# One-layer S5 trunk: 1/rms interleaved with the powers, decays ahead of the outer products, three pools opened in another order

## The chip, the core and the metric

The kernel runs on one core of a Trainium2 chip. It has a matrix engine (TensorE, PE in the rows), a vector engine (VectorE, DVE), an engine for functions of one input (ScalarE, ACT), GpSimd (POOL), and queues that issue DMAs: most are issued by SyncE (SP), some by GpSimd. Each engine works through its own instructions in the order in which they stand. The metric is the device time of one execution in microseconds (us); lower is better.

## The reference

With DEPTH = 1 there is one layer on 2048 frames of 1024 values: an S5 mixer, a squared-ReLU MLP, a gate with a per-layer input embedding, and a last norm.

```python
def rmsnorm(x, gain):  # x * rsqrt(mean(x*x) + 1e-6) * gain

h = rmsnorm(x, norm_mix)
# S5, for each of 64 groups of 16 channels, 64 complex states:
#   a = exp(lam*dt);  state[t] = a*state[t-1] + B u[t];  y = Re(C state) + d*u
y = gelu(s5(h));  a, g = split(y @ w_glu)
x = x + a * sigmoid(g)
x = x + relu(rmsnorm(x, norm_ffn) @ w1)**2 @ w2
x = x + (p @ ple_w) * sigmoid(rmsnorm(x, norm_ple) @ ple_gate_w)
return rmsnorm(x, norm_final)
```

All is float32. Large products run as three products of a high and a low part each: the high part is a cast by ScalarE (`h_`), the low part a subtraction by VectorE (`l_`).

## The kernel before

The 2048 frames are two halves of 1024 (`hb` 0 and 1), the channels eight octets of 8 groups. The stages, in order of time:

- **Prologue.** VectorE works out a, its powers 1 to 8 (`pw_r`, `pw_i`, lines 410 to 423) and from power 8 the decays `al[:, 0]`; `stat_steps` (line 180) gives 1/rms of half 0 from sums of squares that ScalarE made, in 14 small instructions on 128x8 values. `decay_steps` (line 434) squares `al` seven times: `sq`, then the real part, then the imaginary part. `scan` reads `al[:, 0]` to `al[:, 6]`.
- **S5 of half 0** (line 882 on). An octet has the outer products `gm` (`make_w`) and `vm` (`make_v`): each is a product with the real powers, one with the imaginary powers, and their sum. VectorE makes them whole (3 instructions of 128x1024) for octets in `W_DVE` and `V_DVE`, GpSimd in halves (6 instructions of 128x512) for the others. `norm` multiplies the frames by 1/rms, `turn` and `turn_w` transpose, `sums` multiplies into `xs`, which lies in PSUM, `scan` runs the recurrence on VectorE. Octets go in pairs: both scans take turns, and the lists `PLAN0` to `PLAN2` say after which step of the scan the other engines' work is issued. `make_k` needs `vm` of its octet. `Ple` is the product of p and `ple_w`, whose pieces (`pp`, `po`) go beside the scans; `rest` makes the low part `plo` of the transposed p.
- **GLU of half 0** with S5 of half 1 beside it, then **the MLP of half 0** (`mlp`): products `up` with w1, then `dn` with w2, each in units that `run` issues with loads and casts some units ahead. Then **the gate** (`gate`). The same for half 1.

The S5 stage and the MLP stand inside `tc.manual_schedule`: the named engines get their instructions in the written order. Outside such a block a scheduler sets the order. It also lets code that is written after the block (the first gate weights `raw_gw`, `w_gw`) stand between the block's instructions.

Buffers come from pools that are opened and closed like a stack, from both ends of SBUF. A pool opened where another was closed takes its memory, and its tiles wait for the last use of the old ones. `open_residual` (line 1544) opens the pools of the second part of the MLP and of the gate over the pools `uw` and `ur` of `up` (`ur` holds the raw w1 blocks `rawu`), at the end of `up`. In half 1 `ur` is opened over these again:

```python
wp = right.enter_context(...)      # 9 x 4 KB, over uw
rawp = right.enter_context(...)    # 4 x 2 KB raw weights of gate and GLU
tmps[-1] = right.enter_context(...)  # 3 x 2 KB
aps.append(right.enter_context(...))  # 7 x 2 KB and 4 KB of g_fin
```

Of the kernel before, what the change touches and what calls it, by code (L numbers as in the profile page):

```python
# [9 lines left out]
F32 = mybir.dt.float32  # L10
# [3 lines left out]
ALU = mybir.AluOpType  # L14
# [16 lines left out]
NOCT = 8  # L31
# [7 lines left out]
def trunk(  # L39
# [24 lines left out]
    pe, dve, act, pool, sp = nc.tensor, nc.vector, nc.scalar, nc.gpsimd, nc.sync  # L64
# [30 lines left out]
    const = ctx.enter_context(tc.tile_pool(name="const", bufs=1))  # L95
# [25 lines left out]

    ident = const.tile([P, P], F32, name="ident")
    make_identity(nc, ident)
    al = const.tile([P, 8, NOCT, 2, 2, 4], F32, name="al")
    carry = const.tile([P, 2, 32], F32, name="carry")
    g_ffn = const.tile([P, KT], F32, name="g_ffn")
    g_ple = const.tile([P, KT], F32, name="g_ple")
# [62 lines left out]
    pr0 = tmp.enter_context(tc.tile_pool(name="pr0", bufs=1, side="right"))  # L190
# [16 lines left out]
    for i, c in enumerate((c_re, c_im)):  # L207
# [9 lines left out]
    sq = small.tile([P, NOCT, 2, 4], F32, name="sq", bufs=1)  # L217
# [6 lines left out]
        out=k_d[:].rearrange("(a b) h r -> (b h) a r", b=8)[:, :, 0:7 * H], in_=zpad)  # L224
# [37 lines left out]
    ss0 = stat_squares(0, xs0[:10])  # L262
# [74 lines left out]
    pw_r = par.tile([P, 9, G], F32, name="pw_r")  # L337
    pw_i = par.tile([P, 9, G], F32, name="pw_i")
# [71 lines left out]
    for lo, n in ((1, 1), (2, 2), (4, 4)):  # L410
        q1 = pr0.tile([P, 4, G], F32, tag="q1", name=f"q1_{lo}", bufs=2)[:, :n]
        q2 = pr0.tile([P, 4, G], F32, tag="q2", name=f"q2_{lo}", bufs=2)[:, :n]
        q3 = pr0.tile([P, 4, G], F32, tag="q3", name=f"q3_{lo}", bufs=2)[:, :n]
        q4 = pr0.tile([P, 4, G], F32, tag="q4", name=f"q4_{lo}", bufs=2)[:, :n]
        ar, ai = pw_r[:, 1:n + 1], pw_i[:, 1:n + 1]
        br = pw_r[:, lo:lo + 1].broadcast_to([P, n, G])
        bi = pw_i[:, lo:lo + 1].broadcast_to([P, n, G])
        mul(q1, ar, br)
        mul(q2, ai, bi)
        mul(q3, ar, bi)  # L420
        mul(q4, ai, br)
        sub(pw_r[:, lo + 1:lo + 1 + n], q1, q2)
        add(pw_i[:, lo + 1:lo + 1 + n], q3, q4)


    for e in range(2):
        ls = slice(e * S, e * S + S)
        pr = pw_r[ls, 8].rearrange("p (o i e) -> p e o i", e=2, i=4)[:, e]
        pi = pw_i[ls, 8].rearrange("p (o i e) -> p e o i", e=2, i=4)[:, e]
        for r_ in range(2):  # L430
            dve.tensor_copy(out=al[ls, 0, :, 0, r_], in_=pr)
            ts(al[ls, 0, :, 1, r_], pi, 1.0 - 2 * r_, ALU.mult)

    def decay_steps():
        for k in range(7):
            re = al[:, k, :, 0]
            mul(sq, al[:, k, :, :, 0], al[:, k, :, :, 0])
            yield
            tt(al[:, k + 1, :, 0], sq[:, :, 0].unsqueeze(2).broadcast_to([P, NOCT, 2, 4]),
               sq[:, :, 1].unsqueeze(2).broadcast_to([P, NOCT, 2, 4]), ALU.subtract)  # L440
            yield
            stt(al[:, k + 1, :, 1], re, 2.0, al[:, k, :, 1], ALU.mult, ALU.mult)
            yield

    rs0 = []
    for _ in stat_steps(0, ss0, rs0):
        pass
    startup.close()
    tmp.close()


    beside = []

    def tick(n=None):

        for _ in range(n or TICK):
            if beside:
                g = beside.pop(0)
                if next(g, StopIteration) is not StopIteration:
                    beside.append(g)  # L460

    W_DVE, V_DVE = (0,), (0, 2, 4, 6)
    TICK = 4

    class Octet:

# [45 lines left out]
        def outer(self, name, sl, za, zb, on_pool):  # L512

            eng = pool if on_pool else dve
            a_ = self.tile(name, (P, 8, 8, H))
            n = 4 if on_pool else 8
            for j in range(0, 8, n):
                js = slice(j, j + n)
                b_ = self.tile(f"{name}b{j}", (P, n, 8, H), tag="pa" if on_pool else "tm")
                for t, w, z in ((a_[:, js], pw_r, za), (b_, pw_i, zb)):  # L520
                    eng.tensor_tensor(out=t, in0=self.powers(w, sl)[:, js], in1=self.spread(z)[:, js], op=ALU.mult)
                    if not on_pool:
                        tick()
# [357 lines left out]
    ples = [Ple(j // 2, j % 2) for j in range(4)]  # L881
    with tc.manual_schedule(engines=MANUAL):
# [64 lines left out]
        Ple.load_weights()  # L947
        ples[0].load()
        ples[1].load()
        Ple.weights()  # L950
        a, b = pairs[0]
        a.make_w()
        b.make_w()
        octs[2].make_w()
        b.make_v()
        a.turn_w()
        ples[0].turn(True)
        a.norm(True)
        beside += [decay_steps()]
        a.turn()  # L960
        b.turn_w()
        b.norm()
        a.sums()
        b.turn()
        b.sums()
        a.make_v()
        while beside:
            tick(1)
        diagonal()
        Ple.weights_rest()  # L970
        ple_rest(0)
# [4 lines left out]
        for k in range(NP):  # L976
            a, b = 2 * k, 2 * k + 1
# [19 lines left out]
        a, b = pairs[-1]  # L997
# [28 lines left out]
    tmps, aps = [], []  # L1026
# [511 lines left out]
    right = ctx.enter_context(ExitStack())  # L1538
# [5 lines left out]
    def open_residual(hb):  # L1544

        nonlocal xp, wp, rawp, g_fin, ps_tp
        tops.close()
        xp = left.enter_context(tc.tile_pool(name=f"xp{hb}", bufs=8, reuse_waits="tile"))
        wp = right.enter_context(tc.tile_pool(name=f"wp{hb}", bufs=9, side="right", reuse_waits="tile"))
        rawp = right.enter_context(tc.tile_pool(name=f"rawp{hb}", bufs=4, side="right", reuse_waits="tile"))  # L1550
        tmps[-1] = right.enter_context(tc.tile_pool(name=f"tp_{hb}", bufs=3, side="right", reuse_waits="tile")), 512
        aps.append(right.enter_context(tc.tile_pool(name=f"ap_{hb}", bufs=7, side="right", reuse_waits="tile")))
        g_fin = aps[-1].tile([P, D], F32, name=f"g_fin{hb}", bufs=1)
        sp.dma_start(out=g_fin, in_=norm_final.partition_broadcast(P))

# [50 lines left out]
```

## Time and profile before

| | us |
|---|---|
| time, median of 3 runs | 2131.78 |
| lowest and highest run | 2127.62 to 2133.33 |
| the profiled execution's own time | 2130.64 |
| its span, first to last instruction | 2128.9 |
| PE busy | 1993.3 (94%) |
| DVE busy | 1387.4 (65%) |
| ACT busy | 887.9 (42%) |
| POOL busy | 427.0 (20%) |

The page names an instruction by its line, engine and operation, then output<-inputs, then the shape and how many were merged into the row. Idle time stands in brackets with what ended it. The mean granted clock of TensorE over the span is 0.984 of full speed. The time outside the span is 2130.64 - 2128.9 = 1.7 us.

### The profile page before, as it was taken

Reading aid. Unit: us, or ns where it says so; the run is one execution under the profiler, and the core shown is the slowest. Engines: PE = TensorE matmul, PEld = TensorE weight load, DVE = VectorE, ACT = ScalarE, POOL = GpSimd, SP = SyncE. Lnnn points to the kernel's source line nnn. Section 1 sums busy time; section 2 is a strip of 40 time slices with the busy share of each in tenths; the row PEclk is TensorE's granted clock in tenths of the full one; section 3 lists DMA queues with packets and bytes.
Section 4 is the critical chain, followed back from the end, with each engine's and each line's share of the span. In section 5 each row is a group of like instructions: output and inputs, shape, how many; then the busy total and the mean of one; then the engine's idle time right before and its main releaser. Section 6 shows DMA issues by size and latency. Waiting matters only on the chain.

```text
span 2128.9 us, 28570 instructions
## 1 busy us (share of the span) xinstructions
PE 1993.3 (94%) x9750; PEld 1655.5 (78%) x9750; DVE 1387.4 (65%) x2592; ACT 887.9 (42%) x1769; POOL 427.0 (20%) x388
## 2 busy tenths in 40 slices
PE   2788989988999999999999999979999999999997
PEld 1677778776888888888888788867888888888876
DVE  9997587759666666875664722377666657555455
ACT  4675444335333345354443511253333355444443
POOL 5563011123322212522300000022322200000000
PEclk9899999999999999999999999989999999999999
DMA  5677644342444469999832711224444598665112
GB/s 169 191 216 208 198 129 139 100 139 84 153 154 161 145 220 354 373 358 344 274 137 79 269 53 40 85 94 153 159 149 159 172 356 303 206 195 192 39 50 89
DMA packets 241955, 377.35 MB, mean 177 GB/s; under 512 B 23681, under 2 KB 106641, under 8 KB 241809
## 3 DMA queue, kind: packets, MB, share of 16 engines
q1 hardware_dynamic: 234576, 352.46, 49.5%
q0 software_dynamic: 7232, 23.08, 3.0%
q8 instruction: 76, 1.25, 0.2%
q14 instruction: 71, 0.57, 0.1%
HBM read 261.21 MB, written 114.23 MB: 176 GB/s over the span
## 4 chain that ended last, share of the span: by engine, by line
PE 72%; DVE 14%; issue 4%; ACT 4%; DMA 3%; POOL 3%; SPq 0%; DVEq 0%; ACTq 0%; POOLq 0%
PE dn L1376 26%; PE up L1284 25%; PE glu L1046 3%; PE glu L1047 3%; PE glu L1048 3%; PE gt L1046 2%; PE gt L1047 2%; PE gt L1048 2%; DVE tm L72 2%; DVE es L72 2%; DVE xs L72 1%; DVE wu L72 1%; DMA rawu<-in_mlp_w_dram 1%; ACT xs L668 1%; PE glu L850 1%
## 5 line engine op out<-in xcount | busy, mean ns | idle before, releaser
L1284 PE MATMUL up<-h_s,wu 128*128 128x512 f32 x1280 | 407.9, 392 | 8.4 <-DVE ev L72 7.9
L1376 PE MATMUL dn<-h_dw,h_da 128*128 128x512 f32 x896 | 349.1, 390 | 0.0
L1376 PE MATMUL dn<-l_dw,h_da 128*128 128x512 f32 x896 | 348.7, 389 | 0.3 <-DVE l_dw L72 0.3
L1376 PE MATMUL dn<-h_dw,l_da 128*128 128x512 f32 x896 | 348.7, 389 | 0.0
L72 DVE TENSOR_TENSOR l_da<-da,h_da 128x512 fp32r<-128x512 f32 x224 | 183.2, 818 | 178.5 <-ACT h_da L1174 178.4
L1284 PEld LDWEIGHTS up<-h_s,wu 128*128 128x128 f32 x1280 | 242.0, 189 | 61.7 <-DVE ev L72 9.2
L1284 PE MATMUL up<-l_s,wu 128*128 128x512 f32 x640 | 251.0, 392 | 12.4 <-DVE l_s L72 12.4
L72 DVE TENSOR_TENSOR wu<-rawu,wu 128x512 fp32r<-128x512 f32 x224 | 164.3, 747 | 112.1 <-ACT wu L1272 111.7
L1174 ACT CAST h_da<-da 128x512 fp32r<-128x512 f32 x224 | 139.0, 621 | 232.8 <-PE dn L1376 211.7
L1046 PE MATMUL glu<-w_glu,ah_y 128*128 128x512 f32 x492 | 196.1, 399 | 6.2 <-ACT w_glu L734 5.2
L1376 PEld LDWEIGHTS dn<-l_dw,h_da 128*128 128x128 f32 x896 | 168.2, 188 | 35.5 <-DVE l_dw L72 0.8
L1047 PE MATMUL glu<-w_glu,ah_y 128*128 128x512 f32 x492 | 193.9, 394 | 1.6 <-DVE w_glu L72 1.6
L1376 PEld LDWEIGHTS dn<-h_dw,h_da 128*128 128x128 f32 x896 | 168.2, 188 | 34.9
L1376 PEld LDWEIGHTS dn<-h_dw,l_da 128*128 128x128 f32 x896 | 168.2, 188 | 34.8
L1270 POOL TENSOR_TENSOR rawu<-rawu,rawu 128x512 f32<-128x512 f32 x96 | 134.2, 1412 | 299.4 <-DVE wu L72 299.4
L1048 PE MATMUL glu<-w_glu,al_y 128*128 128x512 f32 x492 | 193.5, 394 | 0.0
L1284 PE MATMUL up<-ah_f,wu 128*128 128x512 f32 x512 | 171.8, 397 | 7.3 <-ACT wu L1272 7.0
L1272 ACT CAST wu<-rawu 128x512 fp32r<-128x512 f32 x224 | 132.2, 620 | 91.4 <-POOL rawu L1270 63.4
L72 DVE TENSOR_TENSOR l_dw<-dw,h_dw 128x512 fp32r<-128x512 f32 x224 | 161.0, 719 | 11.0 <-ACT h_dw L1174 9.3
L1295 ACT COPY ev<-up 128x512 f32<-128x512 f32 x96 | 56.3, 586 | 247.0 <-PE up L1284 247.0
L1174 ACT CAST h_dw<-dw 128x512 fp32r<-128x512 f32 x224 | 138.1, 617 | 48.5 <-POOL dw L1361 45.8
L1284 PEld LDWEIGHTS up<-l_s,wu 128*128 128x128 f32 x640 | 121.0, 189 | 38.9 <-DVE l_s L72 14.2
(309 smaller groups left out, 3334.9 us busy)
## 6 DMA issues: line engine op xcount, KB each, us to landing
da<-h_d SPq DMA_DIRECT2D x224, 256.0 KB, 5.0
dw<-in_mlp_w_dram SPq DMA_DIRECT2D x192, 256.0 KB, 5.1
rawu<-in_mlp_w_dram SPq DMA_DIRECT2D x64, 512.0 KB, 3.8
h_d<-ev SPq DMA_DIRECT2D x96, 256.0 KB, 2.1
h_d<-hs SPq DMA_DIRECT2D x96, 256.0 KB, 2.1
dw<-t_d SPq DMA_DIRECT2D x96, 256.0 KB, 4.7
t_d<-dw SPq DMA_DIRECT2D x64, 256.0 KB, 5.1
raw_glu<-in_ssm_w_glu_dram SPq DMA_DIRECT2D x59, 256.0 KB, 4.5
```

Of the source, the lines that this page charges most:

```text
L72: return dve.tensor_tensor(out=o, in0=a, in1=b, op=op)
L668: act.copy(dd[c * S:(c + 1) * S, :, e], self.es[e * S:(e + 1) * S, c])
L850: pe.matmul(out=pf, lhsT=lhs[:, cs_], rhs=wl if i == 1 else wh, start=k == 0 and i == which[0], stop=False)
L1046: pe.matmul(out=ps, lhsT=lh, rhs=rh, start=first, stop=False)
L1047: pe.matmul(out=ps, lhsT=lh, rhs=rl, start=False, stop=False)
L1048: pe.matmul(out=ps, lhsT=ll, rhs=rh, start=False, stop=last)
L1174: act.copy(h_, src)
L1270: pool.tensor_tensor(out=src, in0=src, in1=other, op=ALU.add)
L1272: act.copy(w_[:, 0], src)
L1284: pe.matmul(out=ps, lhsT=lhs, rhs=rhs, start=i in FIRST_IN_CHAIN and k == n == 0, stop=k == 3 and n == 2, skip_group_check=True)
L1295: act.copy(ev[g, i], y_ if i == 5 else x_)
L1376: pe.matmul(out=ps, lhsT=lhs[:, cs_], rhs=rhs, start=i in FIRST_IN_CHAIN and fp == n == 0, stop=fp == NPAIR - 1 and n == 2, skip_group_che ...
```

## The change

Four things are changed in the prologue, and one further on.

1. The six instructions per power round and the 14 of 1/rms take turns on VectorE (`power_steps`, `stat_steps`), instead of powers, then `al[:, 0]`, then 1/rms.
2. The decays (`decays`) are written before all outer products, and not a few at a time between VectorE's outer products by `tick`. They end at `al[:, 6]`; `al` is one entry smaller. The real part of the last one is made by GpSimd, which thus stands ahead of GpSimd's first outer product. Two copies of `al[:, 0]` become one for each half of the lanes.
3. Octet 0 is normalized by ScalarE and not by VectorE, and this, the transposes of p and of octet 0 stand before `turn_w` of octet 0 (and so before `gm` of octet 0 is waited for) on ScalarE and TensorE. The casts of `ple_w` (`plwh`) stand after octet 1's `turn_w`.
4. In `open_residual` the pool of 7 buffers `ap_` is opened ahead of `rawp` and `tp_`.

```diff
-    al = const.tile([P, 8, NOCT, 2, 2, 4], F32, name="al")
+    al = const.tile([P, 7, NOCT, 2, 2, 4], F32, name="al")
...
+    def decays():
+        for e in range(2):
...
+            dve.tensor_copy(out=al[ls, 0, :, 0], in_=pr.unsqueeze(2).broadcast_to([S, NOCT, 2, 4]))
+            for r_ in range(2):
+                ts(al[ls, 0, :, 1, r_], pi, 1.0 - 2 * r_, ALU.mult)
+        for k in range(6):
             mul(sq, al[:, k, :, :, 0], al[:, k, :, :, 0])
+            stt(al[:, k + 1, :, 1], al[:, k, :, 0], 2.0, al[:, k, :, 1], ALU.mult, ALU.mult)
+            (pool if k == 5 else dve).tensor_tensor(
+                out=al[:, k + 1, :, 0], in0=sq[:, :, 0].unsqueeze(2).broadcast_to([P, NOCT, 2, 4]),
+                in1=sq[:, :, 1].unsqueeze(2).broadcast_to([P, NOCT, 2, 4]), op=ALU.subtract)
 
-    for _ in stat_steps(0, ss0, rs0):
-        pass
+    with tc.manual_schedule(engines={mybir.EngineType.Activation, mybir.EngineType.DVE}):
+        steps_ = [power_steps(), stat_steps(0, ss0, rs0)]
+        while steps_:
+            steps_ = [g for g in steps_ if next(g, StopIteration) is not StopIteration]
...
-        Ple.weights()
         a, b = pairs[0]
+        decays()
         a.make_w()
         b.make_w()
         octs[2].make_w()
         b.make_v()
+        a.norm()
+        ples[0].turn(True)
+        a.turn()
         a.turn_w()
-        ples[0].turn(True)
-        a.norm(True)
-        beside += [decay_steps()]
-        a.turn()
+        b.norm()
         b.turn_w()
-        b.norm()
+        Ple.weights()
         a.sums()
...
         wp = right.enter_context(tc.tile_pool(name=f"wp{hb}", bufs=9, side="right", reuse_waits="tile"))
+        aps.append(right.enter_context(tc.tile_pool(name=f"ap_{hb}", bufs=7, side="right", reuse_waits="tile")))
         rawp = right.enter_context(tc.tile_pool(name=f"rawp{hb}", bufs=4, side="right", reuse_waits="tile"))
         tmps[-1] = right.enter_context(tc.tile_pool(name=f"tp_{hb}", bufs=3, side="right", reuse_waits="tile")), 512
-        aps.append(right.enter_context(tc.tile_pool(name=f"ap_{hb}", bufs=7, side="right", reuse_waits="tile")))
```

VectorE in the prologue, from the first outer product of octet 0 on, before (`gm`, `vm`: outer products of octet 0; `xn_0`: its normalized frames; `y_x`: 1/rms; `sq`, `al`: decays):

```order
L521 TENSOR_TENSOR gm_0_546<-pw_r,zz 128x1024
L89 SCALAR_TENSOR_TENSOR y_x_505<-q_x_502,y_x_500 128x8
L521 TENSOR_TENSOR gmb_0_0_547<-pw_i,zz 128x1024
L524 TENSOR_TENSOR gm_0_546<-gm_0_546,gmb_0_0_547 128x1024
L85 TENSOR_SCALAR xn_0_605<-xl_0_514,y_x_505 128x8x16 x8
L521 TENSOR_TENSOR vm_0_695<-pw_r,y_199 128x1024
L72 TENSOR_TENSOR sq<-al 128x64
L72 TENSOR_TENSOR al<-sq 128x8x8
L89 SCALAR_TENSOR_TENSOR al<-al 128x8x8
L72 TENSOR_TENSOR sq<-al 128x64
L521 TENSOR_TENSOR vmb_0_0_696<-pw_i,y_200 128x1024
```

The same place of the changed kernel, from the last decays on:

```order
L89 SCALAR_TENSOR_TENSOR al<-al 128x8x8
L445 TENSOR_TENSOR al<-sq 128x8x8
L72 TENSOR_TENSOR sq<-al 128x64
L89 SCALAR_TENSOR_TENSOR al<-al 128x8x8
L517 TENSOR_TENSOR gm_0_553<-pw_r,zz 128x1024
L517 TENSOR_TENSOR gmb_0_0_554<-pw_i,zz 128x1024
L518 TENSOR_TENSOR gm_0_553<-gm_0_553,gmb_0_0_554 128x1024
L517 TENSOR_TENSOR vm_0_714<-pw_r,y_199 128x1024
L517 TENSOR_TENSOR vmb_0_0_715<-pw_i,y_200 128x1024
L518 TENSOR_TENSOR vm_0_714<-vm_0_714,vmb_0_0_715 128x1024
```

The eight instructions of `xn_0` are gone from VectorE, and no decay stands between the outer products. GpSimd's six instructions each for `gm_1`, `gm_2` and `vm_1` stand as before, but behind one `al<-sq` that waits for VectorE's last `sq`.

SyncE in half 1, where the GLU ends and the MLP begins, before (`raw_glu_b_k`: raw GLU weights of block b; `rawu`: raw w1 blocks):

```order
L1037 DMA raw_glu_3_5_12340<-in_ssm_w_glu_dram 128x2x256
L1037 DMA raw_glu_3_6_12345<-in_ssm_w_glu_dram 128x2x256
L1037 DMA raw_glu_3_7_12350<-in_ssm_w_glu_dram 128x2x256
L1257 DMA rawu_0_0_12696<-in_mlp_w_dram 128x4x256
L1257 DMA rawu_0_1_12698<-in_mlp_w_dram 128x4x256
L1257 DMA rawu_1_0_12700<-in_mlp_w_dram 128x4x256
L1257 DMA rawu_1_1_12702<-in_mlp_w_dram 128x4x256
```

And in the changed kernel, a block and a half of weights earlier:

```order
L1027 DMA raw_glu_2_3_12048<-in_ssm_w_glu_dram 128x2x256
L1247 DMA rawu_0_0_12694<-in_mlp_w_dram 128x4x256
L1027 DMA raw_glu_2_4_12053<-in_ssm_w_glu_dram 128x2x256
L1247 DMA rawu_0_1_12696<-in_mlp_w_dram 128x4x256
L1247 DMA rawu_1_0_12698<-in_mlp_w_dram 128x4x256
L1247 DMA rawu_1_1_12700<-in_mlp_w_dram 128x4x256
L1027 DMA raw_glu_2_5_12058<-in_ssm_w_glu_dram 128x2x256
```

The four loads of the first two w1 blocks moved ahead of eleven loads of GLU weights; `ur` now lies over buffers of `ap_`.

SyncE in half 0, where the MLP ends and the gate begins, before (`raw_gw`: raw gate weights; six of the first eight stand some 300 instructions earlier; `ppl`: pieces of p's product):

```order
L1362 DMA t_d_103<-dw_0_4_15_10157 128x512
L1037 DMA raw_gw_0_6_10615<-in_ple_gate_w_dram 128x512
L1037 DMA raw_gw_0_7_10620<-in_ple_gate_w_dram 128x512
L1453 DMA ppl_0_0_10625<-pp_d 128x512
L1453 DMA ppl_0_1_10659<-pp_d 128x512
```

And in the changed kernel:

```order
L1352 DMA t_d_103<-dw_0_4_15_10155 128x512
L1027 DMA raw_gw_0_0_10583<-in_ple_gate_w_dram 128x512
L1027 DMA raw_gw_0_1_10588<-in_ple_gate_w_dram 128x512
L1027 DMA raw_gw_0_2_10593<-in_ple_gate_w_dram 128x512
L1027 DMA raw_gw_0_3_10598<-in_ple_gate_w_dram 128x512
L1443 DMA ppl_0_0_10623<-pp_d 128x512
L1443 DMA ppl_0_1_10657<-pp_d 128x512
L1027 DMA raw_gw_0_4_10603<-in_ple_gate_w_dram 128x512
L1027 DMA raw_gw_0_5_10608<-in_ple_gate_w_dram 128x512
L1027 DMA raw_gw_0_6_10613<-in_ple_gate_w_dram 128x512
L1027 DMA raw_gw_0_7_10618<-in_ple_gate_w_dram 128x512
```

All eight raw gate weights of the first block now stand here, behind the last load and store of the MLP; ScalarE's casts and VectorE's subtractions of them moved along. In half 1 they stand among the loads of the sixth of the seven `dn` products.

## Rows read from the trace of the kernel before

**Rows 1.** The page, busy time of the engines (share of the span, instructions).
```profile
PE 1993.3 (94%) x9750; PEld 1655.5 (78%) x9750; DVE 1387.4 (65%) x2592; ACT 887.9 (42%) x1769; POOL 427.0 (20%) x388
```

**Rows 2.** Windows of 50 us: busy time (instructions) by engine, granted clock, DMA.
```profile
50.00:100.00 50.00, 34.47 (x276) 28.84 (x278) 49.45 (x127) 26.83 (x65) 25.79 (x23) 0.89 0.57 155
...
1650.00:1700.00 50.00, 50.00 (x223) 41.39 (x222) 32.19 (x49) 16.44 (x30) 11.57 (x9) 1.00 0.48 161
```

**Rows 3.** Timeline of VectorE, 18 to 210 us: start, duration, instruction, shape, count.
```profile
30.69 0.42 DVE L72 TENSOR_TENSOR pw_i<-q,q 128x256 f32<-128x256 f32 x1
...
35.02 1.03 DVE L86 TENSOR_SCALAR v_x<-s 128x8 f32<-128x8 f32 x1
...
48.70 2.01 DVE L524 TENSOR_TENSOR gm<-gm,gmb 128x1024 f32<-128x1024 f32 x1
50.63 5.41 DVE L85 TENSOR_SCALAR xn<-xl,y_x 128x128 f32<-128x128 f32 x8
55.96 1.21 DVE L521 TENSOR_TENSOR vm<-pw_r,y 128x1024 f32<-128x1024 f32 x1
57.09 0.21 DVE L72 TENSOR_TENSOR sq<-al 128x64 f32<-128x64 f32 x1
...
57.73 0.23 DVE L72 TENSOR_TENSOR sq<-al 128x64 f32<-128x64 f32 x1
...
62.10 1.04 DVE L72 TENSOR_TENSOR sq<-al 128x64 f32<-128x64 f32 x1
...
70.48 2.49 DVE L72 TENSOR_TENSOR plwl<-plw,plwh 128x512 fp32r<-128x512 f32 x4
...
74.09 2.34 DVE L72 TENSOR_TENSOR tm<-al,xs 128x1024 f32<-128x1024 f32 x2
...
84.74 1.28 DVE L72 TENSOR_TENSOR plo<-tpp,ph 128x512 fp32r<-128x512 f32 x2
...
93.03 2.31 DVE L72 TENSOR_TENSOR tm<-al,xs 128x1008 f32<-128x1008 f32 x2
...
207.83 0.17 DVE L85 TENSOR_SCALAR h_x<-v_x 128x8 int32<-128x8 int32 x1
```

**Rows 4.** Timeline of GpSimd, 30 to 95 us.
```profile
31.42 1.11 POOL L521 TENSOR_TENSOR gm<-pw_r,zz 128x512 f32<-128x512 f32 x1 [14.21 <-ACT y L386]
...
45.35 2.16 POOL L521 TENSOR_TENSOR vm<-pw_r,y 128x512 f32<-128x512 f32 x1
...
54.04 1.32 POOL L524 TENSOR_TENSOR vm<-vm,vmb 128x512 f32<-128x512 f32 x1
...
82.94 0.60 POOL L815 DMA_DIRECT2D pp_d<-po  x1 [15.07 <-ACT po L813]
...
93.55 1.28 POOL L524 TENSOR_TENSOR vm<-vm,vmb 128x512 f32<-128x512 f32 x1
```

**Rows 5.** Timeline of ScalarE, 59 to 84 us.
```profile
59.58 2.45 ACT L491 ACTIVATE xn<-xl,y_x 128x128 f32<-128x128 f32 x8
...
82.55 1.07 ACT L795 CAST ph<-tpp 128x512 fp32r<-128x512 f32 x2
```

**Rows 6.** Timeline of TensorE where `up` begins: half 0, then half 1.
```profile
467.67 1.04 PE L1067 MATMUL tpx_f<-ident,x 128*128 128x128 f32 x8
...
475.16 1.91 PE L1213 MATMUL tpu<-ident,x 128*128 128x128 f32 x16
...
1381.85 1.04 PE L1067 MATMUL tpx_f<-ident,x 128*128 128x128 f32 x8
1388.46 0.80 PE L1284 MATMUL up<-ah_f,wu 128*128 128x512 f32 x1 [5.57 <-ACT wu L1272]
...
1393.48 1.91 PE L1213 MATMUL tpu<-ident,x 128*128 128x128 f32 x16
```

**Rows 7.** Timeline of SyncE's queue and of TensorE at the gate of half 0.
```profile
1074.62 0.91 SPq L1037 DMA_DIRECT2D raw_gw<-in_ple_gate_w_dram  x2
...
1106.44 0.47 PE L1046 MATMUL gt<-w_gw,ah_g 128*128 128x512 f32 x1
```

**Rows 8.** The tile `raw_gw`: us from the issue of a load to its landing.
```profile
DMA to landing us min/median/max: 2.5/4.5/6.8
```

More of the change, by code (lines that the diff above doesn't have):

```diff
@@ L407, in diagonal @@
         mul(dg, dl.unsqueeze(2).broadcast_to([P, H, H]), mask16.unsqueeze(1).broadcast_to([P, H, H]))
[L410 to L423, printed above, removed]
@@ L426, in trunk, with power_steps @@
[L426 to L436, printed above, removed]
-            mul(sq, al[:, k, :, :, 0], al[:, k, :, :, 0])
[L438 to L443, printed above, removed]
+    def power_steps():
+        for lo, n in ((1, 1), (2, 2), (4, 4)):
+            q1 = pr0.tile([P, 4, G], F32, tag="q1", name=f"q1_{lo}", bufs=2)[:, :n]
+            q2 = pr0.tile([P, 4, G], F32, tag="q2", name=f"q2_{lo}", bufs=2)[:, :n]
+            q3 = pr0.tile([P, 4, G], F32, tag="q3", name=f"q3_{lo}", bufs=2)[:, :n]
+            q4 = pr0.tile([P, 4, G], F32, tag="q4", name=f"q4_{lo}", bufs=2)[:, :n]
+            ar, ai = pw_r[:, 1:n + 1], pw_i[:, 1:n + 1]
+            br = pw_r[:, lo:lo + 1].broadcast_to([P, n, G])
+            bi = pw_i[:, lo:lo + 1].broadcast_to([P, n, G])
+            mul(q1, ar, br)
+            yield
+            mul(q2, ai, bi)
+            yield
+            mul(q3, ar, bi)
+            yield
+            mul(q4, ai, br)
+            yield
+            sub(pw_r[:, lo + 1:lo + 1 + n], q1, q2)
+            yield
+            add(pw_i[:, lo + 1:lo + 1 + n], q3, q4)
+            yield
@@ new lines, in decays @@
+    def decays():
+        for e in range(2):
+            ls = slice(e * S, e * S + S)
+            pr = pw_r[ls, 8].rearrange("p (o i e) -> p e o i", e=2, i=4)[:, e]
+            pi = pw_i[ls, 8].rearrange("p (o i e) -> p e o i", e=2, i=4)[:, e]
+            dve.tensor_copy(out=al[ls, 0, :, 0], in_=pr.unsqueeze(2).broadcast_to([S, NOCT, 2, 4]))
+            for r_ in range(2):
+                ts(al[ls, 0, :, 1, r_], pi, 1.0 - 2 * r_, ALU.mult)
+        for k in range(6):
+            mul(sq, al[:, k, :, :, 0], al[:, k, :, :, 0])
+            stt(al[:, k + 1, :, 1], al[:, k, :, 0], 2.0, al[:, k, :, 1], ALU.mult, ALU.mult)
+            (pool if k == 5 else dve).tensor_tensor(
+                out=al[:, k + 1, :, 0], in0=sq[:, :, 0].unsqueeze(2).broadcast_to([P, NOCT, 2, 4]),
+                in1=sq[:, :, 1].unsqueeze(2).broadcast_to([P, NOCT, 2, 4]), op=ALU.subtract)
@@ L445, in trunk @@
     rs0 = []
-    for _ in stat_steps(0, ss0, rs0):
-        pass
+    with tc.manual_schedule(engines={mybir.EngineType.Activation, mybir.EngineType.DVE}):
+        steps_ = [power_steps(), stat_steps(0, ss0, rs0)]
+        while steps_:
+            steps_ = [g for g in steps_ if next(g, StopIteration) is not StopIteration]
     startup.close()
     tmp.close()
[L452 to L460, printed above, removed]
@@ L462, in trunk @@
     W_DVE, V_DVE = (0,), (0, 2, 4, 6)
-    TICK = 4
     class Octet:
@@ L521, in outer @@
                     eng.tensor_tensor(out=t, in0=self.powers(w, sl)[:, js], in1=self.spread(z)[:, js], op=ALU.mult)
-                    if not on_pool:
-                        tick()
                 eng.tensor_tensor(out=a_[:, js], in0=a_[:, js], in1=b_, op=ALU.add)
-                if not on_pool:
-                    tick()
             return a_
@@ L966, in trunk @@
         a.make_v()
-        while beside:
-            tick(1)
         diagonal()
```

## The prediction

> **What bounds the kernel now.** The first view to read is the page's line of busy times: TensorE works 94% of the span, VectorE 65% [rows 1]. A share of 94% says that most edits on other engines are worth nothing, and that a gain must come from the stretches in which TensorE waits. The windows of 50 us show which these are. From 1650 to 1700 TensorE is busy for all 50.00 us; from 50 to 100, in the S5 stage of half 0, it is busy for 34.47 and VectorE for 49.45 [rows 2]. There VectorE is the bound, and TensorE's later work starts when VectorE has its scans done. So a microsecond taken from VectorE ahead of its first scan step (`tm` at 74.09) is a microsecond of the whole, as long as nothing else comes late at that scan.
>
> The third view is VectorE's timeline of that stretch, read beside GpSimd's. VectorE's busy time there is partly not its own. The tiny 1/rms instruction at 35.02 takes 1.03 where one of the same shape takes 0.17 at 207.83; a decay `sq` takes 1.04 at 62.10 and 0.21 at 57.09; a sum `gm` 2.01 at 48.70, a product of that size 1.21 at 55.96; and the eight pieces of `xn` 5.41 at 50.63 [rows 3], which ScalarE makes for the next octet in 2.45 [rows 5]. GpSimd was at its outer products then, and its own instruction took 2.16 at 45.35 where the first took 1.11 [rows 4]. 2.16 is 1.11 and about one product of VectorE: the two engines take turns, one whole instruction each. An instruction that reads xs in PSUM is not touched: `tm` takes 2.31 for two at 93.03, with GpSimd's sum at 93.55 beside it, and 2.34 at 74.09 [rows 3, 4]. So a small VectorE instruction costs 1 us, not 0.2, wherever GpSimd has a product waiting, and moving the small ones ahead of GpSimd's first product is the core of this change.
>
> The Trainium skill (SBUF — State Buffer, section Who interferes with whom) says that a VectorE instruction with two SBUF inputs contends with a GpSimd instruction that reads SBUF, that the pair of ports is held for the full instruction, and that at most one SBUF input outside the 2-port modes doesn't contend; the slow `gm` and the untouched `tm` above agree. By this rule the products of the two engines never lie beside each other, wherever the change puts them, which speaks against it; what follows from that for the time is the first rival, worked out from rows there.
>
> **Part 1, the prologue.** Powers end at 31.11 (`pw_i` at 30.69, 0.42) [rows 3]. The 14 instructions of 1/rms now stand between those of the powers. Bounds: nothing, if they fill the gaps between dependent instructions, and 14 x 0.17 = 2.4; I take 1.4, nearer the upper one, since the queue is one: 32.5. `al[:, 0]` is six instructions of 0.17, 1.0: 33.5. A decay step of three is 0.64 (57.09 to 57.73) [rows 3]; five steps and two thirds of a sixth are 3.6: 37.1. GpSimd starts there and not at 31.42 [rows 4], 5.7 later; nothing on VectorE is slowed until then, and for that time GpSimd is the one that pays.
>
> From 37.1 VectorE has to do, before the first scan step: six outer products at 1.13 (55.96 to 57.09), 6.8; five small ones of the carry and the diagonal, 1.0; four `plwl` at 2.49/4, 2.5; two `plo` at 1.28/2, 1.3, with an operand in PSUM [rows 3]: 11.6 in all. Fifteen of these read two SBUF operands, and between them fourteen GpSimd instructions of 1.11 pass if turns are taken: 15.5. The scan then starts at 37.1 + 11.6 + 15.5 = 64.2 rather than 74.09, 9.9 earlier. Bounds: all eighteen GpSimd products (`gm_1`, `gm_2`, `vm_1`, six each) pass first, 20.0, and it starts at 68.7, a gain of 5.4; or the five small and the four `plwl` yield nothing, and it starts near 59, a gain of 15. The value is the turns, since 2.16 and 1.04 are each one turn.
>
> What is late next: `xn_0` now is ScalarE's, 2.45, and ScalarE is busy for 26.83 of 50 us there [rows 2], so the work fits; but it stands ahead of the copies and casts that follow. `vm_1` is next: GpSimd needs 20.0 and VectorE's turns of 10.3, so it ends near 67.5, against 55.36 before (54.04 and 1.32) [rows 4], and so from 18.7 ahead of the scan's start to 3 behind it. `make_k` of octet 1 stands behind it on TensorE and ScalarE, and behind that the copies `ph`, which ended at 83.62 for a `plo` at 84.74 [rows 3, 5]: a margin of 1.1. I put VectorE's new wait at 1.5, between 0 (if `make_k` catches up in TensorE's idle third) and 3 (the lateness without the margin). GpSimd itself was idle for 15.07 before its next task at 82.94 [rows 4], so its later start hands nothing on there. Net of the prologue: 9.9 - 1.5 = 8.4 gained; bounds 4 and 15.
>
> **Part 2, the start of the second MLP.** In half 1 `up` has a wait of 5.57 for ScalarE's cast `wu`, whose raw block came late because `ur` lay over pools freed only at the end of the GLU. From the first `tpx_f` to `tpu` TensorE needs 11.63 there (1381.85 to 1393.48) and 7.49 in half 0 (467.67 to 475.16), where nothing was late [rows 6]. Now the four `rawu` loads stand eleven GLU loads earlier, and the casts can be done beside the GLU. If half 1 becomes as half 0: 11.63 - 7.49 = 4.1 gained. If the wait goes and what follows it is not lengthened: 5.57. The products behind the wait, in the 5.02 from 1388.46 to 1393.48, are slow: the first takes 0.80, where `gt` of the same shape takes 0.47 at 1106.44 [rows 6, 7]. If they go at that rate as well, 5.02 becomes 2.9, and 5.57 + 2.1 = 7.7 is gained. I take 6.4, between the last two, because in half 1 the GLU that runs up to this place keeps TensorE at work, with no idle time ahead of `up` to lower its clock. Behind this place all of the MLP shifts.
>
> **Part 3, the gate weights.** The gate's raw loads of half 0 were issued in part some 300 instructions early; now all eight stand behind the last load of `dn`, in two rounds of four buffers. The issue of the two that stood there before was at 1074.62, and the first `gt` at 1106.44 [rows 7], 31.8 later. A load lands after 4.5, 6.8 at most [rows 8]. Two rounds with a cast and a subtraction each need about 2 x (6.8 + 3) = 20. I cost it at 0, hidden by the end of `dn`; bound: 1 lost. In half 1 they stand among the loads of the sixth `dn` product, a whole product ahead of use, beside a TensorE that is never idle [rows 2]: 0. The loads and casts that leave their old place give nothing back either, for the same reason.
>
> **The sum.** The profiled execution took 2130.64: its span of 2128.9 and 1.7 around it. 2130.64 - 8.4 - 6.4 = 2115.8; the median of the runs is 1.1 above that execution, so 2116.9, and I say 2117.
>
> **Rivals.**
> 1. GpSimd becomes the bound. If its products win more than every other turn, or if the delay of `vm_1` is handed on whole, the prologue gives 4 to 5 (scan start near 68.7, or 64.2 and a wait of 5). For it: GpSimd starts 5.7 later with the same 20.0 of work. Against: the turns in the rows are one for one, and VectorE's outer products are of its own queue. Total 4.5 + 6.4 = 10.9, time 2121.
> 2. The second MLP starts no better than half 0's, or waits for another late part (the casts stand behind the GLU's on ScalarE). For it: half 0's 7.49 is a measured start without such a wait. Part 2 then gives 0 to 4.1, the time is 2119 to 2123.
> 3. The small instructions do not yield to GpSimd, for which only the 0.21 of 57.09 speaks [rows 3]: prologue 13 to 15, time 2111.
> 4. Slower: the gate weights. In half 0 two landing rounds must pass between the loads and `gt`. It would stall from the point where a round (load, cast, subtraction) takes over 31.8/2 = 16, and to outweigh the 14.8 gained a round has to take about 23 at this gate alone, over three times the longest landing of 6.8 [rows 8]. Time then 2132 and more.
> 5. The change doesn't do what it says: `ur` overlaps a tile freed no earlier, and part 2 is nothing (the order of SyncE's queue shows the loads moved, not that they don't wait). It is in rival 2's upper end.
>
> **How the numbers follow.** The forecast has 0.60, rival 1 0.18, rival 2 with 5 0.12, rival 3 0.07, rival 4 0.03. The forecast's own range is 2113 to 2121 (its two terms by 3 each way); with the rivals, 2109 to 2125 leaves out less than 2 in 10. A measurement of this kernel tells about 0.3%, 6.4 us, from no change. All of the cases but the fourth are over 8.9 us faster, and 2125 is the bound; both parts at their lower ends (4 and 0) would be within it: 0.05. So faster 0.92, same 0.05, slower 0.03.
>
> **What would show it.** In the changed profile: the 1/rms rows of VectorE at 0.1 to 0.2 rather than 1.03; GpSimd's first `gm` near 37; the first `tm` near 64, and `vm_1` ended near 67; `xn_0` on ScalarE at 2.45; a wait of at most 2 before the `plo` of the first scan; in half 1 no wait for `wu` and 4 to 6 us from `tpx_f` to `tpu`; the first `gt` as far behind the last `dn` as before. Wrong it would be if the first `tm` comes at 68 or later, if VectorE waits for TensorE or ScalarE in the first pair of octets for longer than 3, or if what is gained at the first scan is no longer there when the GLU of half 0 begins.

## The result, and the profile after

The changed kernel takes 2109.71 us (median of 4, 2107.2 to 2111.71); the kernel before took 2132.07 (median of 4, 2127.62 to 2133.33). The ratio is 0.9898, interval 0.9884 to 0.9912: 22.4 us faster. The forecast was 2117 with a range of 2109 to 2125, so the time lies 0.7 inside its lower end, and one of the four executions (2107.2) lies below it. The profiled execution took 2109.95, 20.7 less than that of before, where the prediction's sum had 14.8.

The page's line of busy times, and the windows that answer to [rows 1] and [rows 2]:

```profile
PE 1996.4 (95%) x9750; PEld 1660.0 (79%) x9750; DVE 1380.3 (65%) x2578; ACT 889.6 (42%) x1777; POOL 431.1 (20%) x389
```

```profile
50.00:100.00 50.00, 40.63 (x402) 35.00 (x403) 47.41 (x104) 33.32 (x82) 44.74 (x39) 0.84 0.69 199
```

VectorE's total is only 7 us smaller, and it is still the busiest engine from 50 to 100. What is new there is GpSimd at 44.74 of 50 (25.79 before) and TensorE at 40.63 (34.47): three engines are now busy for 81 to 95% of this stretch. VectorE's timeline, whose rows answer to [rows 3]:

```profile
27.33 0.17 DVE L86 TENSOR_SCALAR v_x<-s 128x8 f32<-128x8 f32 x1
...
33.42 0.23 DVE L72 TENSOR_TENSOR sq<-al 128x64 f32<-128x64 f32 x1
...
37.16 2.13 DVE L517 TENSOR_TENSOR gmb<-pw_i,zz 128x1024 f32<-128x1024 f32 x1
39.33 2.01 DVE L518 TENSOR_TENSOR gm<-gm,gmb 128x1024 f32<-128x1024 f32 x1
...
47.56 1.23 DVE L72 TENSOR_TENSOR carry<-carry 128x16 f32<-128x16 f32 x1
...
52.46 6.30 DVE L72 TENSOR_TENSOR plwl<-plw,plwh 128x512 fp32r<-128x512 f32 x4
...
59.88 2.33 DVE L72 TENSOR_TENSOR tm<-al,xs 128x1024 f32<-128x1024 f32 x2
...
72.89 1.29 DVE L72 TENSOR_TENSOR plo<-tpp,ph 128x512 fp32r<-128x512 f32 x2 [2.19 <-ACT ph L787]
...
81.25 2.31 DVE L72 TENSOR_TENSOR tm<-al,xs 128x1008 f32<-128x1008 f32 x2
```

The reader is to see that the price of a turn has moved. 1/rms (`v_x`) and the decays (`sq`) are now at 0.17 and 0.23. The outer products pay instead: five of the six, which took 1.21 or 1.22 before with one at 2.01, now take 2.01 to 2.29. So do a tiny `carry`, at 1.23, and the low parts of ple_w, `plwl`, at 6.30/4 = 1.58 rather than 0.62. Still the first `tm` stands at 59.88 rather than 74.09, 14.2 earlier; a new wait of 2.19 follows in the scan, and the last large step comes 11.8 earlier (81.25 for 93.03). GpSimd, for [rows 4]:

```profile
35.85 0.30 POOL L445 TENSOR_TENSOR al<-sq 128x64 f32<-128x64 f32 x1 [18.64 <-DVE sq L72]
36.18 2.02 POOL L517 TENSOR_TENSOR gm<-pw_r,zz 128x512 f32<-128x512 f32 x1
...
48.72 1.10 POOL L517 TENSOR_TENSOR gm<-pw_r,zz 128x512 f32<-128x512 f32 x1
...
63.27 1.27 POOL L518 TENSOR_TENSOR vm<-vm,vmb 128x512 f32<-128x512 f32 x1
```

Its products take 2.02 to 2.13 beside VectorE's large ones and 1.10 beside the small ones. `vm_1` ends at 64.54, 9.2 later than before and 4.7 behind the scan's start. TensorE at the start of the second MLP, for [rows 6], and the gate of half 0, for [rows 7]:

```profile
1368.66 1.04 PE L1057 MATMUL tpx_f<-ident,x 128*128 128x128 f32 x8
...
1369.90 0.47 PE L1274 MATMUL up<-ah_f,wu 128*128 128x512 f32 x1 [0.20 <-ACT wu L1262]
...
1373.29 1.91 PE L1203 MATMUL tpu<-ident,x 128*128 128x128 f32 x16
```

```profile
1093.03 0.47 PE L1036 MATMUL gt<-w_gw,ah_g 128*128 128x512 f32 x1
```

The wait of 5.57 is 0.20, the first `up` takes 0.47 rather than 0.80, and `tpx_f` to `tpu` is 4.63 rather than 11.63: 7.0 gained, of which 5.4 are the wait and 1.6 the matmuls behind it (3.39 rather than 5.02). The first `gt` is 13.4 earlier.

The last view is a table made from two traces: the same matmul is looked up in both (TensorE's matmuls from there on stand in the same sequence, counted from the end), and the difference of the starts, each counted from the start of its span as in the rows, is the lead over the kernel before. A lead that stays the same over a stretch says that no time is gained or lost there.

| place (time in the kernel before) | changed | pools only | prologue only |
|---|---|---|---|
| S5 of half 0, 145 to 170 | 11.0 | 0.1 | 11.6 |
| `up` of half 0, 600 | 12.8 | 0.1 | 12.1 |
| `dn` of half 0, 900 | 13.4 | 0.7 | 12.3 |
| GLU of half 1, 1360 | 13.2 | 0.3 | 8.3 |
| `up` of half 1, 1600 | 20.3 | 7.4 | 5.4 |
| `dn` of half 1, 2000 | 20.7 | 7.8 | 4.5 |

### The profile page after: what moved, and what is told of

Read it like the earlier page. It is cut to its first block, busy times and chain, and to the rows that moved or that the text cites. A ratio compares the mean times of both kernels' runs of the same rounds, so it can differ in the third digit from the quotient of the medians.

```text
span 2108.2 us, 28567 instructions
## 1 busy us (share of the span) xinstructions
PE 1996.4 (95%) x9750; PEld 1660.0 (79%) x9750; DVE 1380.3 (65%) x2578; ACT 889.6 (42%) x1777; POOL 431.1 (20%) x389
## 4 chain that ended last, share of the span: by engine, by line
PE 75%; DVE 11%; issue 4%; POOL 4%; ACT 3%; DMA 2%; SPq 0%; DVEq 0%; ACTq 0%; POOLq 0%
PE dn L1366 29%; PE up L1274 26%; PE glu L1037 3%; PE glu L1036 3%; PE glu L1038 3%; DVE tm L72 3%; PE gt L1038 2%; PE gt L1036 2%; PE gt L1037 2%; DVE es L72 2%; DVE xs L72 2%; DVE wu L72 1%; ACT xs L660 1%; POOL gm L518 1%; POOL gmb L517 1%
## 5 line engine op out<-in xcount | busy, mean ns | idle before, releaser
L1274 PE MATMUL up<-l_s,wu 128*128 128x512 f32 x640 | 251.7, 393 | 12.3 <-DVE l_s L72 12.3
L72 DVE TENSOR_TENSOR l_dw<-dw,h_dw 128x512 fp32r<-128x512 f32 x224 | 167.3, 747 | 13.3 <-ACT h_dw L1164 12.0
L1274 PEld LDWEIGHTS up<-l_s,wu 128*128 128x128 f32 x640 | 121.4, 190 | 39.0 <-DVE l_s L72 14.2
```

The costliest lines, as they stand in the source:

```text
L1274: pe.matmul(out=ps, lhsT=lhs, rhs=rhs, start=i in FIRST_IN_CHAIN and k == n == 0, stop=k == 3 and n == 2, skip_group_check=True)
```

## The experiments

Each was timed with the kernel before on the same chip; its median there was 2131.85 for the first eight, 2131.9 for the next three and 2130.07 for the last one. Leads are those of the profiled execution.

**Pools only.** The kernel before, with `ap_` opened ahead of `rawp` and `tp_`.

> The kernel before with the order of the three pools alone changed. Theory (two independent gains): the prologue is as before, first tm of the scan at 74.1 us; in half 1 the wait of 5.6 for wu is gone and tpx_f to tpu is 4.5 to 5 us rather than 11.63; the end is 7.0 to 7.5 us earlier, 2125. Rival (the weights of the second MLP came in time only because the prologue gave the queues more room, or both gains share one cause): 0 to 3 us, 2129 to 2132.

Measured: 2122.81, ratio 0.9955 (0.9942 to 0.9967). TensorE where the second MLP begins:

```profile
1381.57 1.04 PE L1067 MATMUL tpx_f<-ident,x 128*128 128x128 f32 x8
1382.81 0.47 PE L1284 MATMUL up<-ah_f,wu 128*128 128x512 f32 x1 [0.20 <-ACT wu L1272]
...
1386.18 1.91 PE L1213 MATMUL tpu<-ident,x 128*128 128x128 f32 x16
```

From `tpx_f` to `tpu` it takes 4.61, and the lead jumps from 0.3 to 7.3 there; the first `tm` stands at 74.10. The gain of part 2 needs nothing of the prologue.

**Prologue only.** The changed kernel with the pools in the old order.

> The changed kernel with the three pools in the old order. Theory (two independent gains): first tm at 59.9 as in the changed kernel, in half 1 the wait for wu of 5.6 and 11.6 us from tpx_f to tpu are back; the end is 13 us earlier than before, 2119. Rival (one depends on the other): the wait for wu stays away, or part of the 13 us is lost by the end of the first half; 2110 or 2124.

Measured: 2119.93, ratio 0.994 (0.9927 to 0.9954). The first `tm` is at 59.88, the wait for `wu` is back at 5.48. 9.0 and 11.9 make 20.9, with both 22.4: two independent gains, as far as the intervals tell. The profiled execution was this kernel's longest (2126.18): its lead is about 12 until 1195 and 8.3 behind it, where TensorE waits at the start of the GLU of half 1 for 6.07,

```profile
1198.36 0.79 PE L1036 MATMUL glu<-w_glu,ah_y 128*128 128x512 f32 x1 [6.07 <-ACT w_glu L726]
```

against 3.93 in the changed kernel, and its first matmul then takes 0.79. Another 2.8 go at 1446 to 1449 (times of the kernel before), where seven matmuls of `up` start 0.4 later each. So the last rows of its column are lower than the median has them.

**Octet 0 normalized by VectorE.** The edit turns `a.norm()` into `a.norm(True)`.

> The changed kernel with octet 0 normalized by VectorE again (8 instructions behind octet 0's gm). Theory (turns: a VectorE instruction with SBUF operands lets one waiting GpSimd product pass, and only 18 products are to pass, 13 of which already do): own time 8 x 0.2 = 1.6 and up to 5 more turns of 0.95, so the first tm comes at 61.5 to 66 rather than 59.9; of this 2.2 goes into the wait for ph that is there anyway, so 0 to 4 us slower, 3 taken: 2113. Rival 1 (it costs what it took before, 5.4): 2115. Rival 2 (hidden, as GpSimd's products set the start of the scan): first tm within 0.5 of 59.9, 2110.

Measured: 2112.14, ratio 0.9908 (0.9895 to 0.9922), which the time alone can't tell from the changed kernel's. VectorE's rows:

```profile
41.27 7.11 DVE L85 TENSOR_SCALAR xn<-xl,y_x 128x128 f32<-128x128 f32 x8
...
66.02 2.33 DVE L72 TENSOR_TENSOR tm<-al,xs 128x1024 f32<-128x1024 f32 x2
...
76.66 1.28 DVE L72 TENSOR_TENSOR plo<-tpp,ph 128x512 fp32r<-128x512 f32 x2
```

The scan starts 6.1 later, at the top of what the turns allow, and the wait for `ph` is gone. The lead is 3.0 smaller at 145 to 170 us and 3.4 at the end. Hidden it is not; nor is it worth the 5.4 that it took before.

**The last decay on VectorE.** With it GpSimd's first product waits for the powers only.

```diff
-            (pool if k == 5 else dve).tensor_tensor(
+            dve.tensor_tensor(
```

> The changed kernel with the last decay instruction on VectorE rather than on GpSimd, so that GpSimd's first product no longer waits for the decays. Theory (turns): GpSimd starts at 32.2 rather than 36.2, the decays yield to its products, all 18 products pass ahead of the scan rather than 13, so the first tm comes near 65, 5 later; vm_1 ends some 4 earlier, so the wait of 2.2 for ph goes; net 2 to 3 us slower than the changed kernel, 2112.5. Rival (GpSimd's work is the bound and its 4 us later start is a loss): the first tm not later than 60.5, wait for ph gone, 2 to 4 us faster, 2106 to 2108.

Measured: 2117.3, ratio 0.9925 (0.9913 to 0.9938). VectorE's rows:

```profile
41.68 1.30 DVE L72 TENSOR_TENSOR sq<-al 128x64 f32<-128x64 f32 x1
...
57.68 1.22 DVE L517 TENSOR_TENSOR vmb<-pw_i,y 128x1024 f32<-128x1024 f32 x1
...
66.74 2.34 DVE L72 TENSOR_TENSOR tm<-al,xs 128x1024 f32<-128x1024 f32 x2
```

GpSimd starts at 32.38 and has `vm_1` done at 54.29, so it can't have been short of time, and yet the first `tm` is 6.9 later. The rival that GpSimd's later start is a loss falls. The rows also show that turns are bounded by the number of products: the decays pay, and from 55 on, when GpSimd has no product left, VectorE's products take 1.22. From the first `al` at 32.0 to `tm` are 34.7; 15.7 is VectorE's own work (11.6, and 4.1 of decays), 1.8 a wait for `plwh`, and 17.2 is left for 18 products, 0.96 each. In the changed kernel 59.88 - 36.02 - 11.6 = 12.3 is left, 13 of them at 0.95. So the one instruction on GpSimd keeps five products from costing a turn: one falls beside `plo` and four behind the start of the scan, where one of VectorE's two operands is in PSUM.

The median is 7.6 above the changed kernel's, where 2 to 3 were expected. The leads don't carry the 6.9 on one for one either: this execution is 3.7 behind the changed kernel at 145 to 170 us (7.3), 0.8 in the MLP of half 0 (12.0), 3.5 in the GLU of half 1 (9.7) and 4.8 at the end.

**The diagonal ahead of the decays.** `diagonal()` moved from behind `a.make_v()` to ahead of `decays()`.

> The changed kernel with the five small instructions of the carry and the diagonal ahead of the decays, and so ahead of GpSimd's first product. Theory (turns): they take 1.1 instead of 4.9, GpSimd starts 1.1 later, and xs of octet 1 is ready near 57, so the first tm comes at 57.2 rather than 59.9; vm_1 still ends at 65, so the wait for ph grows from 2.2 to about 5 and the end does not move: 2109 to 2111. Rival (VectorE alone bounds this stage): the wait for ph stays at 2.2, 2.7 to 3.8 faster, 2106.

Measured: 2111.83, ratio 0.9911 (0.9897 to 0.9925). VectorE's rows:

```profile
52.34 6.33 DVE L72 TENSOR_TENSOR plwl<-plw,plwh 128x512 fp32r<-128x512 f32 x4 [3.52 <-ACT plwh L760]
...
59.79 2.33 DVE L72 TENSOR_TENSOR tm<-al,xs 128x1024 f32<-128x1024 f32 x2
...
74.37 1.29 DVE L72 TENSOR_TENSOR plo<-tpp,ph 128x512 fp32r<-128x512 f32 x2 [3.86 <-ACT ph L787]
```

The small ones took 1.4 rather than 4.9 (32.08 to 33.4), and all of it went into a wait of 3.52 that I had not seen: `plwh` stands behind the copies of `gm_1` on ScalarE, and so behind GpSimd's first products. The end is not earlier, as the theory said, though not by the way it said.

**`ph` early.** In the first pair's plan `fill` stands first and `rest` at step 6 of the scan.

> The changed kernel with the transposes and casts of the second half of p (tpp, ph) ahead of make_k of octets 0 and 1, and plo after step 6 of the scan rather than 16. Theory (the wait of 2.2 for ph is the one thing that the late vm_1 costs): the wait is gone, nothing else is late before the second pair, lead over the kernel before 2.2 more from there on: 2107.5. Rival (the wait moves on to kt, or to xs of octet 2): lead not more than 0.5 changed, 2109.7.

Measured: 2110.66, ratio 0.991 (0.9895 to 0.9924), as the rival said. The wait for `ph` is gone and the first pair's scan ends 2.35 earlier, but VectorE waits for the next pair:

```profile
92.59 1.22 DVE L72 TENSOR_TENSOR tm<-al,xs 128x1024 f32<-128x1024 f32 x1 [3.52 <-PE xs L594]
```

Followed back, TensorE's `xs` waits for ScalarE, and ScalarE's copies of the scanned xs (`dd`) stand behind five `po`, each of which waits for a product `pp` of TensorE:

```profile
87.22 0.59 ACT L805 COPY po<-pp 128x512 f32<-128x512 f32 x1 [0.77 <-PE pp L804]
87.70 0.20 ACT L666 COPY dd<-pw_i 128x4 f32<-128x4 f32 x1
```

The scan had ended at 83.6, and the last of these `po` is done at 87.8, where the changed kernel has it at 86.2. So 2.35 earlier became 0.33 at the next pair's first `tm` (92.59 for 92.92).

**Both.** The two edits together.

> Both edits: diagonal ahead of the decays, and ph ahead of make_k. Theory (turns, and the chain of vm_1, make_k, ph taken off the scan): first tm at 57.2, no wait for ph, the sum with kt at step 10 of the scan waits up to 1.5 for make_k of octet 1; first pair ends 3.5 to 5 earlier than in the changed kernel, 2105. Rival (kt, which needs vm_1, takes the place of the wait for ph): first pair ends at most 2.2 earlier, 2107.5.

Measured: 2112.92, ratio 0.9918 (0.9904 to 0.9931). The first `tm` is at 59.70 (the wait of 3.52 for `plwh` again), and the second pair waits 3.19 for `xs`. Neither of the two sides foresaw that.

**Quarters.** The same, with GpSimd's products of octets 1 and 2 in four pieces.

> As the run before, and GpSimd's outer products of octets 1 and 2 in quarters (128x256) rather than halves. Theory (turns: one VectorE instruction waits for one GpSimd instruction, whatever its size): a turn costs 0.5 rather than 0.95, large VectorE products take about 1.6 to 1.7 instead of 2.0 to 2.3; octet 1's gm is ready no earlier, so the first tm stays at 56.5 to 57.5; vm_1 ends 1 to 2 later through 18 more instructions; time within 2 of the run before. Rival (the engines share the port by bytes and not by instructions): VectorE's products still take 2.0 and more.

Measured: 2114.92, ratio 0.9929 (0.9915 to 0.9942). VectorE, then GpSimd:

```profile
38.26 1.67 DVE L517 TENSOR_TENSOR gmb<-pw_i,zz 128x1024 f32<-128x1024 f32 x1
```

```profile
46.88 0.64 POOL L517 TENSOR_TENSOR gm<-pw_r,zz 128x256 f32<-128x256 f32 x1
```

VectorE's product waits 1.67 - 1.13 = 0.54 for a GpSimd instruction that takes 0.64 alone, and 2.13 - 1.13 = 1.0 for one that takes 1.10. A turn is one instruction, not a share of bytes. `gm_1` came no earlier for it: with smaller pieces VectorE has more of the turns, and `plwl` waits 6.56 for `plwh`.

**Products of p later.** `ph` early, and three of the five `pp` and `po` behind the sums of octet 3.

> As the run with ph early, and three of the five products of p (pp, and their copies po on ScalarE) that stood ahead of ScalarE's copies of the scanned xs are issued behind the sums of octet 3. Theory (after the change ScalarE's queue, with po ahead of the copies dd that set xs free, holds the second pair of octets): the two waits for xs at the start of the second pair (3.5 and 1.5) fall to under 1, its first tm comes at 90 to 91 rather than 92.6 to 92.9; about 2 us ahead of the changed kernel there, 2108. Rival (TensorE's products themselves are the bound): the first tm of the second pair not before 92.

Measured: 2116.82, ratio 0.9931 (0.9919 to 0.9944). The second pair starts at 88.78 with one wait of 1.08, about as the theory said; then `plo` of that pair waits 2.69 for `ph`, and the lead is 5.5 smaller than the changed kernel's at 145 to 170 us.

**All early.** This, the diagonal ahead of the decays, and `plwh` ahead of `turn_w` of octet 1.

> As the run before, with the diagonal ahead of the decays and the casts plwh ahead of turn_w of octet 1. Theory: no wait for plwh, first tm at 56.5 to 57.5 rather than 59.9; first pair ends near 81, first tm of the second pair at 87.5 to 89; 4 to 5 us ahead of the changed kernel there, time 2105. Rival (octet 1's gm, which GpSimd makes from its first product on, holds xs of octet 1): first tm at 59 and later, gain as in the run before.

Measured: 2113.83, ratio 0.9922 (0.9908 to 0.9935). The first `tm` is at 56.34 and the second pair starts 5.0 earlier than in the changed kernel; yet on TensorE the three products come first, and then

```profile
99.09 0.49 PE L679 MATMUL y<-vm,dd 128*128 128x128 f32 x2 [3.15 <-ACT kt L564]
```

where the changed kernel has its first `y` at 97.12. At 145 to 170 us the lead is 4.0 smaller than the changed kernel's.

**1/rms in a row.** Behind the powers instead of in turn with them.

> The changed kernel with 1/rms behind the powers instead of in turn with them, still ahead of the decays. Theory (the gain of part 1 is that 1/rms stands ahead of GpSimd's first product, not that it takes turns with the powers): the 14 instructions take 2.0 to 2.9 rather than 1.1, since each waits for the one before; the decays and GpSimd start 1 to 2 later, the first tm at 61 to 62. Rival (the turns carry the gain): first tm at 65 and later.

One execution: 2112.0, first `tm` at 61.40, 1.5 later, and a lead 1.9 to 2.1 smaller down to the end. The turns with the powers are worth that; the rest is the place ahead of GpSimd's products.

**Products at step 37.** All early, with the three products at step 37 of the second pair's scan.

> The run with all early parts, but the three products of p that were moved stand at step 37 of the second pair's scan, and not ahead of that pair's ph and kt. Theory (what the run with all early parts had won at the start of the second pair was given back because those products stood ahead of ph on TensorE and ScalarE): first tm of the second pair at 87.5 to 89 again, no wait for ph there, the third pair 3 to 5 us ahead of the changed kernel, 2105 to 2107. Rival (TensorE's and ScalarE's own work of the stage, not VectorE's, now sets its end, so that what is moved is given back somewhere else): first tm of the second pair at 88, but the lead is under 1.5 by the end of the stage (GLU of half 0), 2109 to 2112.

Measured: 2111.22, ratio 0.9916 (0.9901 to 0.9932), as the rival said. VectorE's rows:

```profile
87.65 1.21 DVE L72 TENSOR_TENSOR tm<-al,xs 128x1024 f32<-128x1024 f32 x1
...
127.99 1.29 DVE L72 TENSOR_TENSOR al_y<-tpy,ah_y 128x512 fp32r<-128x512 f32 x2 [5.69 <-ACT ah_y L733]
```

5.3 ahead at the second pair, VectorE then waits 5.69 for ScalarE, whose copies stand behind products of p from TensorE, and the lead is 3.6 behind the changed kernel's at 165 us and 1.6 behind in the MLP of half 0. The windows from 100 to 200, changed kernel first, then this one:

```profile
100.00:200.00 100.00, 87.21 (x731) 75.16 (x730) 88.64 (x269) 62.92 (x139) 49.09 (x47) 0.98 0.75 211
```

```profile
100.00:200.00 100.00, 86.16 (x721) 74.19 (x721) 79.81 (x241) 64.14 (x141) 47.65 (x47) 1.00 0.76 205
```

VectorE is busy for 8.8 less in that stretch, but the stretches don't hold the same work: it has 28 instructions fewer in this one. What tells more is its waits for ScalarE from 100 to 170: 14.1 in all here, 3.7 in the changed kernel. VectorE thus has room there and TensorE's products come no sooner; that ScalarE and TensorE set the pace is what the waits suggest, and no run shows it by itself. None of these versions beats the changed kernel.

## Why the prediction was right, and where its sizes were off

*The mechanism of part 1* held: small instructions ahead of GpSimd's first product cost 0.17 to 0.23, and nearly all that stands beside the products yields one turn each. The term was mis-sized, 9.9 for the first `tm` where 14.2 was measured. Of the 4.3, 1.1 is the start: the decays ended at 36.0 and not at 37.1, since the 14 instructions of 1/rms took 1.1 in the gaps of the powers rather than 1.4, and `al` and the decays 3.9 rather than 4.6. The other 3.2 are the turns: 12.3 rather than 15.5, thirteen at 0.95 rather than fourteen at 1.11. I took GpSimd's whole instruction as the price, and a turn is shorter; and one of two `carry` passed free. That "a small VectorE instruction costs 1 us, not 0.2, wherever GpSimd has a product waiting" was too strong, as the trace of before shows: three of the instructions of 1/rms took 0.17 beside GpSimd, each as GpSimd went from its second product to the sum that needs it.

```profile
37.14 0.17 DVE L139 CAST hf_x<-h_x 128x8 f32<-128x8 int32 x1
```

```profile
35.98 1.10 POOL L521 TENSOR_TENSOR gmb<-pw_i,zz 128x512 f32<-128x512 f32 x1
37.16 1.27 POOL L524 TENSOR_TENSOR gm<-gm,gmb 128x512 f32<-128x512 f32 x1
```

*What comes late next* was named rightly: `vm_1`, `make_k` and `ph`, at 1.5 where 2.19 was measured; and `vm_1` at 64.5, not 67.5. But the wait did not cost its length: with `ph` early it went, and the second pair began 0.33 earlier, since ScalarE's copies of the products of p were done later still. The net of part 1 was 11.0 at 145 us where 8.4 was forecast. That a microsecond ahead of the first scan is one of the whole holds only roughly: 14.2 at the first `tm` were 11.8 at the last large step and 11.0 at 145 us, and the last decay on VectorE lost 6.9 at the first `tm` and 3.7 at 145 us.

*Part 2* was 6.4 and measured 7.0, with the pools alone too. *Part 3* was 0 for the loads, and that held: the first `gt` is as far ahead as the work in front of it (13.4 both). Something came back that I had denied, with the pools alone as well: 0.6 by the start of `dn` in half 0, and 0.4 late in `up` of half 1, where TensorE's wait for VectorE (`ev`) is 0.78 rather than 1.19. That it comes from the loads that left their old place is not shown.

*What no step of the sum had* are the gains and losses at later borders. By the leads the 20.7 are 11.0 of part 1, 7.0 of part 2 and 2.7 between them and behind them, 1.8 of it from 145 us to the MLP of half 0. Those are no fixed amount: over that stretch the diagonal ahead of the decays gains 5.4, the last decay on VectorE 4.7, the prologue alone 0.4. In part they are waits (the GLU's of 3.93 or 6.07), in part TensorE's clock, which fell at other borders from trace to trace. The changed kernel waits 2.77 at the same place of both halves, and the first matmul behind it takes 0.79 in one and 0.50 in the other:

```profile
512.88 0.79 PE L1274 MATMUL up<-h_s,wu 128*128 128x512 f32 x1 [2.77 <-DVE ev L72]
...
1425.26 0.50 PE L1274 MATMUL up<-h_s,wu 128*128 128x512 f32 x1 [2.77 <-DVE ev L72]
```

The granted clock from 505 to 532 is 0.94 here, 1.00 in the kernel before and 0.87 with the prologue alone. What decides it stays open. So these 2.7 can't be credited to an edit, and without them the time would have been nearer the forecast: that it lies where it does within the range is in part luck.

*The rivals.* Rival 1, that GpSimd's products win more than every other turn, is refuted by the rows (12.3 of waits, not 20), and the delay of `vm_1` was not handed on whole either (a wait of 2.19, not 5). Rival 2 is refuted by the 7.0, which lies above its 0 to 4.1, and with it rival 5, since the pools alone gain as much. Rival 3, that the small instructions yield nothing, has the time closest to the measured one (2111), but by luck: its condition is refuted by the `carry` at 1.23 and the `plwl` at 1.58, and the 14.2 at the first `tm`, inside its 13 to 15, came about by an earlier start and shorter turns. The Trainium skill's rule (SBUF — State Buffer, section Terms), that the port pair is held for the full instruction, agrees with the turns of 0.54 and 1.0; that it makes the products' place worthless does not follow, as five of them now pass beside `plo` and a scan that read one operand from PSUM. The exception for one SBUF input, which the prediction takes from the same page of the Trainium skill (section Who interferes with whom), holds for `tm`, and not for `xn` and `v_x`, which paid with one tensor operand; whether these run in a 2-port mode no run shows. Rival 4's gate weights were nowhere late.

## What to carry to other kernels

Where two engines yield to each other by whole instructions, count turns, not busy time: the tiny instructions are what the other engine's work makes dear, and they belong ahead of its first one, while its work belongs beside instructions that showed no wait, here those with one of two operands in PSUM. One instruction given to the slower engine can hold it back at the right moment. After a gain of ten microseconds, ask which engine is the bound now before the next edit: here three were busy for 81 to 95%, and seven further versions that moved or split work within this stage gained nothing.

## What the runs showed of the hardware

A turn costs the waiting engine somewhat less than the other's instruction takes alone: 0.54 for 0.64 and 1.0 for 1.10 between large products, 1.03 - 0.17 = 0.86 for 1.10 where a 1/rms instruction waits. Over eighteen products, of which GpSimd's take 1.10 to 1.27 alone, it was 17.2, or 0.96 each. An instruction with one tensor operand in SBUF pays as well: eight `xn` took 7.11 beside six of GpSimd's products and 5.41 beside four in the kernel before, where ScalarE takes 2.48 for the same. `tm`, with one operand in SBUF and one in PSUM, paid nothing: 2.31 to 2.34 for two, with GpSimd at its products or not.

From 170 us on, TensorE's first 128x512 matmul after a wait of 5.5 to 6.2 took 0.79 or 0.80 in every trace. After waits of 2.4 to 4.7 it took 0.49 to 0.66 in some and 0.79 or 0.80 in others: 0.49 after 3.93 in the changed kernel, 0.79 after 3.74 at the same place with the last decay on VectorE. So here the length of the wait alone doesn't tell whether the clock falls to the lower of its two levels. The granted clock from 1380 to 1400 was 0.83 in the kernel before, 1.00 with the pools alone. A few microseconds of waiting at a border thus can cost more than their length, and not in the same place in every version.
